# A fourth seven-product pair in the gate and up units of a decoder layer, part of its low halves made by accumulating DMA

## The chip, the cores and the metric

The kernel runs on one core of a Trainium2 chip. The metric is the device time of one execution in microseconds (us); lower is better. A core has a matrix engine (TensorE, in the rows PE; its weight loads are PEld), a vector engine (VectorE, DVE), a scalar engine (ScalarE, ACT), a general engine (GpSimd, POOL) and a queue engine (SyncE, SP). Each takes its own instructions in the order in which the program lists them. They wait for each other by semaphores. Data comes from device memory by DMA, which SP, POOL or ACT start. A kernel keeps its data in an on-chip memory of 128 partitions, and matmuls write into 8 banks of a second memory, each 128 x 512 in fp32.

## What is computed

One decoder layer for 256 rows of width 2048: two token mixers in parallel, an output projection with a residual, and a SwiGLU block (width 5632) with a residual. What the change touches is the SwiGLU block:

```python
h = x + merged_mixers @ w_out
hn = rms_norm(h) * norm_ffn
g, u = hn @ w_ffn_gate, hn @ w_ffn_up          # 2048 x 5632 each
y = h + (silu(g) * u) @ w_ffn_down             # 5632 x 2048
```

All is fp32. Products are made on TensorE in a rounded format, three matmuls for one product: `a_hi*w_hi + a_hi*w_lo + a_lo*w_hi`. A `hi` is a rounded copy, and `lo` is the value minus its `hi`.

## The kernel before

The output projection and the SwiGLU block run as a list (`stream`) of items of class `Pair`, line 1027. A pair is two blocks of 128 rows of two weight columns of 512: four blocks `raw[:, 0..3]`, 1 MB, loaded by two DMAs on SP (`load`, 512 KB each). A **plain** pair (`mm_plain`) multiplies them with the two halves of the rows in 8 products, 24 matmuls. A **seven-product** pair (`mm_seven`) first makes four sums of blocks on VectorE (lines 1052 to 1055) and needs 7 products, 21 matmuls: m1, m2, m3 on the blocks themselves, m4 to m7 on the sums.

`split` makes the operands. A plain pair has one part: `hi` of 2048 columns on ScalarE (line 1060), then `lo` on VectorE (line 1062). A seven-product pair has two parts: three raw blocks (1536 columns), and the four sums (2048). Parts are numbered; a part writes one of four pairs of `hi8`/`lo8` buffers in turn, so it has to wait until TensorE is done with the part four places before it. `run_ffn`, called once ahead of each item, queues loads and parts, so that at most four parts (`PARTS`), those of the running item among them, stand ahead.

A **gate/up unit** (`gate_up(f, hooks)`, f = 0 to 10) is 8 pairs, one pair of rows of the weights after the other, for 512 columns of gate and of up. Pairs 0, 2 and 4 are seven-product ones (`SH`; in f = 0 only 0 and 2). A **down unit** multiplies the product of three or four gate/up units with `w_ffn_down`. The order is f = 0 to 3, two down units of 6 pairs, f = 4 to 7, two down units, f = 8 to 10, two down units.

The banks: m1, m5, m7, m6 take the four `acc` banks; m2, m4, m3 and the bank `c` of the plain pairs take the four others (tag `m`). After the last seven-product pair of a unit `combine` (lines 1118 to 1122) reads the `acc` banks on ScalarE and VectorE; its last instruction is the last to read m5. At the unit's end `last` (line 1131, four instructions) adds the other four banks, and these are free for the next unit only then. In the next unit's first pair m2 is the fifth product, after 12 matmuls. For gate/up, ScalarE applies Silu (1212) and VectorE multiplies (1214).

The product of unit f is transposed for the down unit by `hid_pair` (8 small matmuls, line 1012, into two `acc` banks, then `put_seven` or `put_plain`, which read them and make `hi` and `lo`). Before, this stands in the middle of item 5 of the unit after. With f counted from its group's start, `put_seven` falls to f = 0, 1 of the first group and 0, 1, 2 of the others.

Of the kernel before, what the change touches and what calls it, by code (L numbers as in the profile page):

```python
# [8 lines left out]
F32 = mybir.dt.float32  # L9
# [45 lines left out]
def hybrid_block(ctx: ExitStack, tc: tile.TileContext, x, norm_attn, w_in, fox_f_bias,  # L55
# [893 lines left out]
    hss = keep.tile([P, NT, 4], F32, name="hss")  # L949
    SH = (0, 2, 4)  # L950

# [31 lines left out]
    def put_seven(dst, b, gains):  # L983

        d0, d1 = (dst[:, o].rearrange("p o t -> p (o t)") for o in range(2))
# [12 lines left out]
        nc.vector.tensor_tensor(fo[:, 3], bo[:, 2], fo[:, 2], op=ALU.add)  # L998
        nc.vector.tensor_tensor(d1[:, 0:512], b, d0[:, 0:512].bitcast(F32), op=ALU.subtract)
        if gains is None:  # L1000
            nc.scalar.activation(d0[:, 512:1024], f, AF.Copy)
        else:
            nc.vector.tensor_copy(d0[:, 512:1024], f)
        nc.vector.tensor_tensor(d1[:, 512:1024], f, d0[:, 512:1024].bitcast(F32), op=ALU.subtract)

# [21 lines left out]
    class Pair:  # L1027
        def __init__(self, unit, kp, seven, srcs, mm, pre=None, mid=None, done=None, need=None):
            self.unit, self.kp, self.seven, self.srcs, self.mm = unit, kp, seven, srcs, mm
            self.pre, self.mid, self.done, self.need = pre, mid, done, need  # L1030
            self.parts = 2 if seven else 1
            self.hold = False
            self.raw = None
            self.op = []
# [32 lines left out]

    def unit(order, sevens, srcs, act, done, need, hooks=None, add=None):

# [17 lines left out]
        def mm_seven(ch):  # L1087
            a = act(ch.kp)
            o0 = a.shape[2] - 7

            for key in ("m1 m2 m3 m5 m7 m6 m4" if seen else "m1 m5 m7 m6 m2 m4 m3").split():
                o, part, slot_ = {"m1": (0, 0, 0), "m2": (1, 0, 1), "m3": (6, 0, 2), "m4": (2, 1, 3),
                                  "m5": (3, 1, 0), "m6": (5, 1, 2), "m7": (4, 1, 1)}[key]
                hi, lo = ch.op[part]
# [19 lines left out]
        def combine():  # L1114

            (t1, t3), (u, w) = ([wk([P, 512], "qs", 4) for _ in range(2)], [p3([P, 512], "q2", 5) for _ in range(2)])
# [86 lines left out]
    def hid_pair(f, a, g):  # L1203
# [43 lines left out]
    for g, (f0, f1) in enumerate(GROUPS):  # L1247
# [54 lines left out]

    def run_ffn(i):

# [3 lines left out]
        while True:  # L1308
# [81 lines left out]
```

## Time and profile before

| what | value |
|---|---|
| time, median of 3 runs | 1435.89 us (1435.48 to 1436.24) |
| the profiled execution's own time | 1435.63 us |
| its span, first to last instruction | 1433.9 us |
| TensorE busy in the span | 1424.8 us (99%), 6757 matmuls |
| VectorE busy | 1135.3 us (79%); 88 to 93% in each 100 us from 800 to 1400 us |
| ScalarE busy | 758.7 us (53%) |
| GpSimd busy | 64.9 us (5%) |
| granted TensorE clock | 1.000 over the span |
| DMA | 287.07 MB, mean 200 GB/s |

The profile is of one execution. A busy TensorE there says only that matmuls overlap: a 512-column matmul lasts 0.39 us in the record while the next one starts 0.23 us after it. What it costs is the distance from one start to the next. Idle time of an engine is listed with what ended it.

### The profile page before, as it was taken

What the parts mean: (1) busy time and instruction counts of PE and PEld (TensorE: products, weight loads), DVE (VectorE), ACT (ScalarE), POOL (GpSimd) and SP (SyncE); (2) the same over time, 40 slices, a digit from 0 to 9 for tenths busy, and PEclk for the clock granted to TensorE, in tenths of its full rate; (3) what the DMA queues carried; (4) which work ended last, traced back from release to release, by engine and by line L of the source; (5) the groups of instructions that cost most, each with busy time, mean ns of one, the idle gap of its engine ahead of it and who ended that gap; (6) DMA issues with size and microseconds to landing.
All of it is one profiled execution on the core that took longest, in us unless ns stands there. A gap on an engine that the chain in (4) does not pass through costs nothing.

```text
span 1433.9 us, 18119 instructions
## 1 busy us (share of the span) xinstructions
PE 1424.8 (99%) x6757; PEld 1197.8 (84%) x6757; DVE 1135.3 (79%) x1458; ACT 758.7 (53%) x945; POOL 64.9 (5%) x82
## 2 busy tenths in 40 slices
PE   9999999999999999999999999999999999999998
PEld 7878888899888888888888888888888888888887
DVE  6785866786677545569898999888999988989985
ACT  5466564455566544445565555455555545455542
POOL 0201010000000000000110000010000000000000
PEclk9999999999999999999999999999999999999999
DMA  7567876457544566667775666578555677865594
GB/s 272 185 197 216 268 239 191 145 147 214 152 119 131 178 191 191 190 215 207 249 238 176 206 205 212 199 206 256 190 184 193 204 217 224 240 200 181 180 269 134
DMA packets 156196, 287.07 MB, mean 200 GB/s; under 512 B 9630, under 2 KB 32764, under 8 KB 155980
## 3 DMA queue, kind: packets, MB, share of 16 engines
q1 hardware_dynamic: 150396, 273.77, 60.2%
q0 software_dynamic: 5536, 11.87, 4.3%
q8 instruction: 53, 0.87, 0.2%
q10 hardware_dynamic: 176, 0.27, 0.1%
q14 instruction: 35, 0.29, 0.1%
HBM read 277.48 MB, written 8.40 MB: 199 GB/s over the span
## 4 chain that ended last, share of the span: by engine, by line
PE 93%; DVE 4%; ACT 1%; issue 1%; POOL 0%; ACTq 0%; POOLq 0%; DVEq 0%
PE m L1083 14%; PE m L1085 14%; PE m L1084 14%; PE acc L194 12%; PE acc L196 12%; PE acc L195 12%; PE acc L1084 3%; PE acc L1085 3%; PE acc L1083 3%; PE acc L1012 1%; DVE lo L172 1%; DVE lo L1062 1%; PE m L546 1%; PE m L547 1%; ACT hi L1060 1%
## 5 line engine op out<-in xcount | busy, mean ns | idle before, releaser
L172 DVE TENSOR_TENSOR lo<-raw,hi 128x1024 fp32r<-128x1024 f32 (+5 forms) x229 | 267.5, 1172 | 139.6 <-ACT hi L171 138.8
L1062 DVE TENSOR_TENSOR lo<-raw,hi 128x2048 fp32r<-128x2048 f32 (+1 forms) x148 | 309.7, 2094 | 40.3 <-ACT hi L1060 40.2
L1060 ACT ACTIVATE hi<-raw 128x2048 fp32r<-128x2048 f32 (+1 forms) x148 | 259.6, 1758 | 131.5 <-PE m L1085 67.1
L194 PE MATMUL acc<-hi,u 128*128 128x512 f32 (+4 forms) x832 | 322.3, 387 | 0.7 <-ACT u L271 0.7
L195 PE MATMUL acc<-lo,u 128*128 128x512 f32 (+4 forms) x832 | 317.0, 381 | 1.4 <-DVE lo L172 1.4
L196 PE MATMUL acc<-hi,u 128*128 128x512 f32 (+4 forms) x832 | 316.9, 381 | 0.0
L171 ACT ACTIVATE hi<-raw 128x1024 fp32r<-128x1024 f32 (+5 forms) x229 | 229.0, 1018 | 145.6 <-PE acc L196 135.5
L195 PEld LDWEIGHTS acc<-lo,u 128*128 128x128 f32 x832 | 156.4, 188 | 27.8 <-DVE lo L172 3.1
L196 PEld LDWEIGHTS acc<-hi,u 128*128 128x128 f32 x832 | 156.2, 188 | 27.7 <-DVE u L272 1.1
L194 PEld LDWEIGHTS acc<-hi,u 128*128 128x128 f32 x832 | 156.3, 188 | 26.2 <-ACT u L271 1.2
L1060 ACT ACTIVATE hi<-sums 128x2048 fp32r<-128x2048 f32 x53 | 101.7, 1918 | 140.7 <-DVE sums L1055 126.1
L1083 PE MATMUL m<-hi,hp 128*128 128x512 f32 x440 | 172.1, 391 | 0.0
L1085 PE MATMUL m<-hi,hp 128*128 128x512 f32 x440 | 171.3, 389 | 0.0
L1084 PE MATMUL m<-lo,hp 128*128 128x512 f32 x440 | 171.2, 389 | 0.0
L1062 DVE TENSOR_TENSOR lo<-sums,hi 128x2048 fp32r<-128x2048 f32 x53 | 121.5, 2292 | 27.2 <-ACT hi L1060 27.2
L1085 PEld LDWEIGHTS m<-hi,hp 128*128 128x128 f32 x440 | 82.6, 188 | 17.2
L1084 PEld LDWEIGHTS m<-lo,hp 128*128 128x128 f32 x440 | 82.7, 188 | 16.8
L1083 PEld LDWEIGHTS m<-hi,hp 128*128 128x128 f32 x440 | 82.6, 188 | 16.9
L1083 PE MATMUL m<-hi,u 128*128 128x512 f32 x215 | 84.1, 391 | 0.0
L1085 PE MATMUL m<-hi,u 128*128 128x512 f32 x215 | 83.7, 389 | 0.0
L1084 PE MATMUL m<-lo,u 128*128 128x512 f32 x215 | 83.7, 389 | 0.0
L1052 DVE TENSOR_TENSOR sums<-raw 128x1024 f32<-128x1024 f32 x53 | 64.5, 1217 | 0.2
(307 smaller groups left out, 1963.6 us busy)
## 6 DMA issues: line engine op xcount, KB each, us to landing
raw<-in_w_in_dram SPq DMA_DIRECT2D x127, 512.0 KB
raw<-in_w_ffn_gate_dram SPq DMA_DIRECT2D x88, 512.0 KB
raw<-in_w_ffn_up_dram SPq DMA_DIRECT2D x88, 512.0 KB
raw<-in_w_ffn_down_dram SPq DMA_DIRECT2D x88, 512.0 KB
raw<-in_w_out_dram SPq DMA_DIRECT2D x32, 512.0 KB
raw<-in_w_in_dram SPq DMA_DIRECT2D x24, 384.0 KB
raw<-in_w_up_fox_dram SPq DMA_DIRECT2D x16, 512.0 KB
raw<-in_w_up_nsa_dram SPq DMA_DIRECT2D x16, 512.0 KB
```

The lines of the kernel that those rows point to most:

```text
L171: nc.scalar.activation(hi[:, :m], ch.raw[:, :m], AF.Copy)
L172: nc.vector.tensor_tensor(lo[:, :m], ch.raw[:, :m], hi[:, :m].bitcast(F32), op=ALU.subtract)
L194: nc.tensor.matmul(o, h, ch.hi[:, j], start=first and j == 0, stop=False)
L195: nc.tensor.matmul(o, h, ch.lo[:, j], start=False, stop=False)
L196: nc.tensor.matmul(o, l, ch.hi[:, j], start=False, stop=last and j == w - 1)
L546: nc.tensor.matmul(o, s, ch.hi[:, j], start=j == 0, stop=False)
L1052: nc.vector.tensor_tensor(s[:, 0:2], w[:, 0].unsqueeze(1).to_broadcast([P, 2, 512]), w[:, 1:4:2], op=ALU.add)
L1060: nc.scalar.activation(h, src, AF.Copy)
L1062: return lambda: nc.vector.tensor_tensor(l, src, h.bitcast(F32), op=ALU.subtract)
L1083: nc.tensor.matmul(o, h, hi, start=n == 0, stop=False)
L1084: nc.tensor.matmul(o, h, lo, start=False, stop=False)
L1085: nc.tensor.matmul(o, l, hi, start=False, stop=n + 1 == total[key])
```

## The change

Gate/up units from f = 1 on get a fourth seven-product pair (6), and their items run in the order 0, 1, 2, 3, 4, 6, 5, 7. Of the four plain pairs left, three (1, 3, 7: `thin`) get half of their low part in another way: ScalarE writes the negated rounded copy of the two up blocks into `lo`, and POOL starts a DMA that adds the weights onto it (512 KB, read a second time). VectorE makes only the other half (1024 columns). The second half of such a pair's matmuls needs what the DMA brings.

The `hi` of the sums is made in two instructions of 1024 columns. In a seven-product pair that isn't a unit's first, `run_ffn` is called once more between the first three products and the rest (`between`), and counts the first part as done. The gate product (line 1237 after) is put two items later. The transposes stand ahead of item 7, no longer in the middle of item 5. `put_seven` makes two differences in one instruction and the first `lo` earlier. Buffers are resized.

```diff
-    SH = (0, 2, 4)
+    SH = (0, 2, 4, 6)
...
     def put_seven(dst, b, gains):
-        nc.scalar.activation(d0[:, 0:512], b, AF.Copy)
-        nc.vector.tensor_tensor(fo[:, 1], bo[:, 1], bo[:, 0], op=ALU.subtract)
-        nc.vector.tensor_tensor(fo[:, 0], bo[:, 3], bo[:, 0], op=ALU.subtract)
-        nc.vector.scalar_tensor_tensor(fo[:, 2], fo[:, 0], -1.0, bo[:, 1], op0=ALU.mult, op1=ALU.subtract)
+        nc.scalar.activation(d0[:, 0:n], b[:, 512 - n:], AF.Copy)
+        nc.vector.tensor_tensor(fo[:, 0:2], bo[:, 1:4:2], bo[:, 0].unsqueeze(1).to_broadcast([P, 2, P]),
+                                op=ALU.subtract)
+        nc.vector.scalar_tensor_tensor(fo[:, 2], fo[:, 1], -1.0, bo[:, 1], op0=ALU.mult, op1=ALU.subtract)
+        nc.vector.tensor_tensor(d1[:, 0:n], b[:, 512 - n:], d0[:, 0:n].bitcast(F32), op=ALU.subtract)
         nc.vector.tensor_tensor(fo[:, 3], bo[:, 2], fo[:, 2], op=ALU.add)
-        nc.vector.tensor_tensor(d1[:, 0:512], b, d0[:, 0:512].bitcast(F32), op=ALU.subtract)
...
             h, l = hi[:, :m], lo[:, :m]
-            nc.scalar.activation(h, src, AF.Copy)
+            if src is self.sums:
+                for o in (0, 2):
+                    nc.scalar.activation(hi[:, o:o + 2], src[:, o:o + 2], AF.Copy)
+            elif self.thin:
+                nc.scalar.activation(lo[:, 0:4:3], src[:, 0:4:3], AF.Copy, scale=-1.0)
+                nc.gpsimd.dma_start(lo[:, 0:4:3], self.srcs[1].rearrange("(k p) n -> p k n", p=P), accum_op=ALU.add)
+                src, h, l = src[:, 1:3], hi[:, 1:3], lo[:, 1:3]
+                nc.scalar.activation(hi, self.raw, AF.Copy)
+            else:
+                nc.scalar.activation(h, src, AF.Copy)
...
+                if key == "m5" and later and ch.between:
+                    ch.between()
...
+            stt(u, bk["m5"], -1.0, u, op0=ALU.mult, op1=ALU.subtract)
             stt(w, bk["m5"], -1.0, t3, op0=ALU.mult, op1=ALU.subtract)
-            stt(u, bk["m5"], -1.0, u, op0=ALU.mult, op1=ALU.subtract)
...
     def swiglu(f):
         def done(c):
...
-            for t in range(NT):
-                nc.vector.scalar_tensor_tensor(c[t, 1], c[t, 1], rh[:, t:t + 1], c[t, 0], op0=ALU.mult, op1=ALU.mult)
+            def mult():
+                for t in range(NT):
+                    nc.vector.scalar_tensor_tensor(c[t, 1], c[t, 1], rh[:, t:t + 1], c[t, 0],
+                                                   op0=ALU.mult, op1=ALU.mult)
             hsrc[f] = [c[t, 1] for t in range(NT)]
+            after.append((here[0] + 2, mult))
...
     def gate_up(f, hooks):
-        unit(range(8), SH if f else SH[:2], lambda kp: [w[kp * 2 * P:(kp + 1) * 2 * P, f * 512:(f + 1) * 512]
+        unit((0, 1, 2, 3, 4, 6, 5, 7) if f else range(8), SH if f else SH[:2], lambda kp: [w[kp * 2 * P:(kp + 1) * 2 * P, f * 512:(f + 1) * 512]
                                                         for w in (w_ffn_gate, w_ffn_up)],
-             lambda kp: hT[kp], swiglu(f), None, hooks)
+             lambda kp: hT[kp], swiglu(f), None, hooks, thin=(1, 3, 7) if f else ())
...
-            gate_up(f, transposes(f - 1, 5) if f > f0 + (1 if g else 0) else
+            gate_up(f, transposes(f - 1, (7, 0)) if f > f0 + (1 if g else 0) else
...
-    def run_ffn(i):
+    def run_ffn(i, halfway=False):
...
-                out_parts = sum(1 for (q, _) in parts[:npart] if q >= i)
+                out_parts = sum(1 for (q, o) in parts[:npart] if q > i or (q == i and not (halfway and o == 0)))
...
+        if i >= ffn:
+            ch.between = lambda i=i: run_ffn(i, True)
+        for at_i, fn in [x for x in after if x[0] <= i]:
+            fn()
```

The first place is VectorE at the end of unit f = 5. `acc` and `F` rows up to `u` are the put, `m` rows are `last`, and `lo` rows are parts of the next unit's first pairs. Before:

```order
L1062 TENSOR_TENSOR lo_1712_8989<-raw_1700_8917,hi_1711_8988 128x1536
L995 TENSOR_TENSOR F_9018<-F_9017 128x128
L996 TENSOR_TENSOR F_9018<-F_9017 128x128
L997 SCALAR_TENSOR_TENSOR F_9018<-F_9018,F_9017 128x128
L998 TENSOR_TENSOR F_9018<-F_9017,F_9018 128x128
L999 TENSOR_TENSOR u_1716_9016<-F_9017,u_1716_9016 128x512
L1004 TENSOR_TENSOR u_1716_9016<-F_9018,u_1716_9016 128x512
L974 TENSOR_TENSOR u_1626_8460<-acc_9028,u_1626_8460 128x512
L1062 TENSOR_TENSOR lo_1721_9048<-sums_8990,hi_1720_9047 128x2048
L1062 TENSOR_TENSOR lo_1723_9076<-raw_1703_8948,hi_1722_9075 128x2048
L1131 TENSOR_TENSOR qs_8972<-m_8829,qs_8972 128x512
```

The same place after, from the last instruction of `combine` on:

```order
L1137 SCALAR_TENSOR_TENSOR q_1731_9101<-acc_8887,qs_9099 128x512
L1074 TENSOR_TENSOR lo_1733_9108<-sums_9077,hi_1732_9107 128x2048
L997 TENSOR_TENSOR F_9143<-F_9142 128x256
L999 SCALAR_TENSOR_TENSOR F_9143<-F_9143,F_9142 128x128
L1000 TENSOR_TENSOR u_1735_9141<-F_9142,u_1735_9141 128x512
L1001 TENSOR_TENSOR F_9143<-F_9142,F_9143 128x128
L1006 TENSOR_TENSOR u_1735_9141<-F_9143,u_1735_9141 128x512
L975 TENSOR_TENSOR u_1637_8515<-acc_9152,u_1637_8515 128x512
L1074 TENSOR_TENSOR lo_1740_9160<-raw_1720_9042,hi_1739_9159 128x1024
L1146 TENSOR_TENSOR qs_9098<-m_8899,qs_9098 128x512
```

The put has moved behind the `lo` of the next unit's first sums, and between it and `last` stands one `lo` of 1024 columns where two of 2048 stood.

The second place is ScalarE at the same end of the unit. Before:

```order
L988 ACTIVATE F_9017<-acc_9011 128x512
L994 ACTIVATE u_1716_9016<-F_9017 128x512
L1001 ACTIVATE u_1716_9016<-F_9018 128x512
L973 ACTIVATE u_1626_8460<-acc_9028 128x512
L1060 ACTIVATE hi_1720_9047<-sums_8990 128x2048
L1060 ACTIVATE hi_1722_9075<-raw_1703_8948 128x2048
L1212 ACTIVATE qs_8972<-qs_8972,rh 128x512
```

After, where the rows of line 1067 are the negated copies ahead of the two accumulating DMAs (of pair 7, and of pair 1 of the next unit):

```order
L1067 ACTIVATE lo_1722_9058<-raw_1709_8960 128x2x512
L1070 ACTIVATE hi_1721_9057<-raw_1709_8960 128x2048
L1072 ACTIVATE hi_1724_9075<-raw_1715_8997 128x1536
L1133 ACTIVATE qs_9098<-acc_8883 128x512
L1065 ACTIVATE hi_1732_9107<-sums_9077 128x1024 x2
L990 ACTIVATE F_9142<-acc_9136 128x512
L996 ACTIVATE u_1735_9141<-F_9142 128x512
L1003 ACTIVATE u_1735_9141<-F_9143 128x512
L974 ACTIVATE u_1637_8515<-acc_9152 128x512
L1067 ACTIVATE lo_1740_9160<-raw_1720_9042 128x2x512
L1070 ACTIVATE hi_1739_9159<-raw_1720_9042 128x2048
L1233 ACTIVATE qs_9098<-qs_9098,rh 128x512
```

Ahead of the put stand three more splits, and the negated copy for the next unit's pair 1, with the DMA that it releases, has come to stand behind the put.

## Rows read from the trace of the kernel before

**Rows 1.** TensorE's waits from 800 us on: for what, us, times, longest
```profile
PE acc L1084 <- DVE lo L1062: 0.4, 1, 0.4
```
**Rows 2.** Unit f = 6: us, busy PE, PEld, DVE, ACT, POOL; clock, DMA, GB/s
```profile
1049.80:1092.20 42.40, 42.40 (x193) 35.20 (x192) 39.74 (x38) 23.09 (x18) 0.00 (x0) 1.00 0.60 199
```
**Rows 3.** TensorE's timeline in unit f = 5: start, us, line, tile, count
```profile
1027.91 0.39 PE L1083 MATMUL acc<-hi,h 128*128 128x512 f32 x1
...
1035.39 1.03 PE L1012 MATMUL acc<-ident,q 128*128 128x128 f32 x8
...
1036.50 0.40 PE L1084 MATMUL m<-lo,hp 128*128 128x512 f32 x1
...
1045.57 0.39 PE L1085 MATMUL m<-hi,hp 128*128 128x512 f32 x1
```
**Rows 4.** VectorE's timeline: a combine, a plain part, the sums of a pair
```profile
990.84 0.68 DVE L1119 TENSOR_TENSOR q<-acc,qs 128x512 f32<-128x512 f32 x1
...
993.49 2.28 DVE L1062 TENSOR_TENSOR lo<-raw,hi 128x2048 fp32r<-128x2048 f32 x1
995.68 1.21 DVE L1052 TENSOR_TENSOR sums<-raw 128x1024 f32<-128x1024 f32 x1
...
998.27 1.75 DVE L1062 TENSOR_TENSOR lo<-raw,hi 128x1536 fp32r<-128x1536 f32 x1
```
**Rows 5.** VectorE's timeline at the end of unit f = 5; brackets: idle before
```profile
1039.75 1.75 DVE L1062 TENSOR_TENSOR lo<-raw,hi 128x1536 fp32r<-128x1536 f32 x1
1041.42 0.28 DVE L995 TENSOR_TENSOR F<-F 128x128 f32<-128x128 f32 x1
...
1042.27 0.29 DVE L998 TENSOR_TENSOR F<-F,F 128x128 f32<-128x128 f32 x1
...
1043.26 0.69 DVE L1004 TENSOR_TENSOR u<-F,u 128x512 fp32r<-128x512 f32 x1
1043.87 0.69 DVE L974 TENSOR_TENSOR u<-acc,u 128x512 fp32r<-128x512 f32 x1
1045.55 2.29 DVE L1062 TENSOR_TENSOR lo<-sums,hi 128x2048 fp32r<-128x2048 f32 x1 [1.00 <-ACT hi L1060]
...
1049.96 1.28 DVE L1131 TENSOR_TENSOR qs<-m,qs 128x512 f32<-128x512 f32 x2
```
**Rows 6.** ScalarE's timeline in the same unit
```profile
1028.15 1.92 ACT L1060 ACTIVATE hi<-raw 128x2048 fp32r<-128x2048 f32 x1 [2.31 <-PE m L1085]
...
1042.59 0.63 ACT L1001 ACTIVATE u<-F 128x512 fp32r<-128x512 f32 x1 [5.30 <-DVE F L998]
1043.13 0.58 ACT L973 ACTIVATE u<-acc 128x512 fp32r<-128x512 f32 x1
1043.61 1.91 ACT L1060 ACTIVATE hi<-sums 128x2048 fp32r<-128x2048 f32 x1
...
1050.68 1.34 ACT L1212 ACTIVATE qs<-qs,rh 128x512 f32<-128x512 f32 x2 [3.36 <-DVE qs L1131]
```
**Rows 7.** Groups of 1024 columns, by line and shape: count, busy us, mean ns
```profile
L171 ACT ACTIVATE hi<-raw 128x1024 fp32r<-128x1024 f32 x179 | 187.1, 1057 | 129.8 <-PE acc L196 125.1 <-issue 1.5 <-ACT hi L171 1.4
...
L172 DVE TENSOR_TENSOR lo<-raw,hi 128x1024 fp32r<-128x1024 f32 x179 | 218.4, 1223 | 124.9 <-ACT hi L171 124.2 <-issue 0.2
```
**Rows 8.** GpSimd's timeline: accumulating DMAs of 256 KB into on-chip memory, issue times
```profile
1367.88 0.88 POOL L1154 DMA_DIRECT2D qs<-hacc  x1 [144.85 <-DVE q L1119]
1369.56 0.87 POOL L1154 DMA_DIRECT2D qs<-hacc  x1 [0.80 <-PE acc L1012]
...
1413.72 0.86 POOL L1154 DMA_DIRECT2D qs<-hacc  x1 [41.51 <-DVE q L1119]
1415.17 0.86 POOL L1154 DMA_DIRECT2D qs<-hacc  x1 [0.58 <-DVE q L1121]
```
**Rows 9.** Line 1154 around 1369.56 us: from issue to landing
```profile
DMA to landing us min/median/max: 8.5/8.5/8.5
```
**Rows 10.** Line 1154 around 1415.17 us: from issue to landing
```profile
DMA to landing us min/median/max: 5.8/5.8/5.8
```

More of the change, by code (lines that the diff above doesn't have):

```diff
@@ L983, in put_seven @@
     def put_seven(dst, b, gains):
+        n = (dst.shape[2] - 4) * P
         d0, d1 = (dst[:, o].rearrange("p o t -> p (o t)") for o in range(2))
@@ L993, in put_seven @@
         fo, bo = (v.rearrange("p (o t) -> p o t", o=4) for v in (f, b))
-        nc.scalar.activation(d0[:, 0:512], b, AF.Copy)
-        nc.vector.tensor_tensor(fo[:, 1], bo[:, 1], bo[:, 0], op=ALU.subtract)
-        nc.vector.tensor_tensor(fo[:, 0], bo[:, 3], bo[:, 0], op=ALU.subtract)
-        nc.vector.scalar_tensor_tensor(fo[:, 2], fo[:, 0], -1.0, bo[:, 1], op0=ALU.mult, op1=ALU.subtract)
+        nc.scalar.activation(d0[:, 0:n], b[:, 512 - n:], AF.Copy)
[3 more added lines that the diff above has]
+        nc.vector.tensor_tensor(d1[:, 0:n], b[:, 512 - n:], d0[:, 0:n].bitcast(F32), op=ALU.subtract)
         nc.vector.tensor_tensor(fo[:, 3], bo[:, 2], fo[:, 2], op=ALU.add)
-        nc.vector.tensor_tensor(d1[:, 0:512], b, d0[:, 0:512].bitcast(F32), op=ALU.subtract)
         if gains is None:
-            nc.scalar.activation(d0[:, 512:1024], f, AF.Copy)
+            nc.scalar.activation(d0[:, n:n + 512], f, AF.Copy)
         else:
-            nc.vector.tensor_copy(d0[:, 512:1024], f)
-        nc.vector.tensor_tensor(d1[:, 512:1024], f, d0[:, 512:1024].bitcast(F32), op=ALU.subtract)
+            nc.vector.tensor_copy(d0[:, n:n + 512], f)
+        nc.vector.tensor_tensor(d1[:, n:n + 512], f, d0[:, n:n + 512].bitcast(F32), op=ALU.subtract)
     def transpose_pair(make, srcs, c, kp, sevens, gains=None, where="tp"):
@@ L1031, in __init__ @@
             self.parts = 2 if seven else 1
-            self.hold = False
-            self.raw = None
+            self.hold = self.thin = False
+            self.raw = self.sums = None
+            self.between = None
             self.op = []
@@ L1066, in free, with unit @@
             self.op = []
-    def unit(order, sevens, srcs, act, done, need, hooks=None, add=None):
+    def unit(order, sevens, srcs, act, done, need, hooks=None, add=None, thin=()):
         hooks = hooks or {}
@@ L1089, in mm_seven @@
             o0 = a.shape[2] - 7
-            for key in ("m1 m2 m3 m5 m7 m6 m4" if seen else "m1 m5 m7 m6 m2 m4 m3").split():
+            later = bool(seen)
+            for key in ("m1 m2 m3 m5 m7 m6 m4" if later else "m1 m5 m7 m6 m2 m4 m3").split():
+                if key == "m5" and later and ch.between:
+                    ch.between()
                 o, part, slot_ = {"m1": (0, 0, 0), "m2": (1, 0, 1), "m3": (6, 0, 2), "m4": (2, 1, 3),
-                                  "m5": (3, 1, 0), "m6": (5, 1, 2), "m7": (4, 1, 1)}[key]
+                                  "m5": (4, 1, 0), "m6": (5, 1, 2), "m7": (3, 1, 1)}[key]
                 hi, lo = ch.op[part]
@@ L1114, in combine @@
         def combine():
-            (t1, t3), (u, w) = ([wk([P, 512], "qs", 4) for _ in range(2)], [p3([P, 512], "q2", 5) for _ in range(2)])
+            (t1, t3), (u, w) = ([wk([P, 512], "qs", 4) for _ in range(2)], [p3([P, 512], "q2", 4) for _ in range(2)])
             tt, stt = nc.vector.tensor_tensor, nc.vector.scalar_tensor_tensor
@@ L1145, in unit @@
                                (lambda kp=kp: need(kp)) if need else None))
+            stream[-1].thin = kp in thin
     def two(w, r0, c0):
@@ L1168, in put_h @@
         k = kp // 2 % 2
-        make = lambda kp: p3([P, 2, 8, P], "h7", len(SH), F32R) if kp in SH else p3([P, 2, 2, T], "hp", 8 - len(SH), F32R)
+        make = lambda kp: (p3([P, 2, 2, T], "hp", 4, F32R) if kp % 2 else p3([P, 2, 7, P], "h7", 2, F32R) if kp < 4
+                           else p3([P, 2, 8, P], "h8", 2, F32R))
         gains = [vecT[:, VF + 2 * kp + o:VF + 2 * kp + o + 1] for o in range(2)]
@@ L1207, in hid_pair @@
                                    where="acc")
+    here = [0]
+    after = []
     def swiglu(f):
         def done(c):
+            c = dict(c)
             for t in range(NT):
                 nc.scalar.activation(c[t, 0], c[t, 0], AF.Silu, scale=rh[:, t:t + 1])
-            for t in range(NT):
-                nc.vector.scalar_tensor_tensor(c[t, 1], c[t, 1], rh[:, t:t + 1], c[t, 0], op0=ALU.mult, op1=ALU.mult)
+            def mult():
+                for t in range(NT):
+                    nc.vector.scalar_tensor_tensor(c[t, 1], c[t, 1], rh[:, t:t + 1], c[t, 0],
+                                                   op0=ALU.mult, op1=ALU.mult)
             hsrc[f] = [c[t, 1] for t in range(NT)]
+            after.append((here[0] + 2, mult))
         return done
@@ L1230, in transposes @@
     def transposes(f, j):
-        return {(j, 1): lambda: [hid_pair(f, o, g_of[f]) for o in range(2)]}
+        return {j if isinstance(j, tuple) else (j, 1): lambda: [hid_pair(f, o, g_of[f]) for o in range(2)]}
     def gate_up(f, hooks):
-        unit(range(8), SH if f else SH[:2], lambda kp: [w[kp * 2 * P:(kp + 1) * 2 * P, f * 512:(f + 1) * 512]
+        unit((0, 1, 2, 3, 4, 6, 5, 7) if f else range(8), SH if f else SH[:2], lambda kp: [w[kp * 2 * P:(kp + 1) * 2 * P, f * 512:(f + 1) * 512]
                                                         for w in (w_ffn_gate, w_ffn_up)],
-             lambda kp: hT[kp], swiglu(f), None, hooks)
+             lambda kp: hT[kp], swiglu(f), None, hooks, thin=(1, 3, 7) if f else ())
     def down_unit(g, i, order, hooks):
@@ L1330, in hybrid_block @@
     for i, ch in enumerate(stream):
+        here[0] = i
         if i < ffn:
@@ L1336, in hybrid_block @@
             run_ffn(i)
+        if i >= ffn:
+            ch.between = lambda i=i: run_ffn(i, True)
+        for at_i, fn in [x for x in after if x[0] <= i]:
+            fn()
+        after[:] = [x for x in after if x[0] > i]
         if ch.need:
```

## The prediction

> **What bounds the kernel now.** I began with TensorE's waits, because only time in which TensorE stands still, or matmuls that go away, can change the end. From 800 us on it waited once, for 0.4 us [rows 1]. So the SwiGLU block lasts as long as its matmuls take to start one after the other: from 1036.50 to 1045.57 us there are 40 distances, 0.2267 us each [rows 3]. Eight transposes take 1036.50 - 1035.39 less one distance, 0.88 us. Next I read the stretch of one whole gate/up unit: 42.40 us, of which VectorE works 39.74 and ScalarE 23.09 [rows 2]. So VectorE has 2.7 us of slack in a unit, and it can't use all of it: 1.00 us of idle time stands in one place ahead of the `lo` of the sums, which waits for ScalarE's `hi` [rows 5]. The reader is to see that TensorE is the bound and VectorE is close behind it. What matters is whether VectorE still delivers on time at each place, not how busy it is on average.
>
> **What the change removes.** Ten units (f = 1 to 10) have one pair more at 21 instead of 24 matmuls: 30 x 0.2267 = 6.80 us. This lies wholly on the path. Against the profiled execution's own time of 1435.63 us it gives 1428.8 if nothing waits.
>
> **VectorE's load.** A seven-product pair costs it 2.59 us of sums [rows 4], 1.67 for the `lo` of 1536 columns (1039.75 to 1041.42) [rows 5] and 2.2 for the `lo` of the sums, 6.46 together; a plain part costs 2.19 (993.49 to 995.68) [rows 4]. A thin part has 1024 columns, mean 1.22 us [rows 7]; starts stand some 0.09 closer than durations, so 1.13. Per unit: one plain part becomes a seven-product pair (+4.27), three become thin (-3.18), net +1.1. The two later changes to the put nearly cancel. So VectorE works some 40.8 us in a unit that now has 180 matmuls and 8 transposes, 41.7 us. On average it fits, if idle time stays under 0.9 us a unit. ScalarE gets three copies of 1024 columns (1.06 each [rows 7]) and one more `hi` pair, about 5 us in all, and has 18 us of slack [rows 2]. Splitting the `hi` of the sums lets its second half end under the `lo` of 1536 columns, so idle time ahead of the `lo` of the sums (1.00 us in [rows 5]) goes; that helps VectorE and costs nothing. The later gate product is 1.3 us of VectorE's work moved to where VectorE is ahead; nobody waits for it until the transposes, six items on.
>
> **The unit's end.** This is the place where I expect the new wait. Part numbers give a closed chain there. Pair 7's part takes the buffer of pair 4's sums, which TensorE leaves when item 5 begins. From that moment, in us:
>
> - 0.24 until ScalarE starts (1027.91 to 1028.15) [rows 3, 6]; 0.95 for the negated copy (1.06 less the overlap); 1.94 from the start of `hi` to VectorE's `lo` (1043.61 to 1045.55) [rows 5, 6]; 1.13 for that `lo`. Sum 4.26.
> - Next unit's pair 0, first part: 2.59 + 1.67. Sum 8.52.
> - `combine` 2.65 (990.84 to 993.49) [rows 4]. Sum 11.17. `lo` of the sums 2.20. Sum 13.37.
> - The put up to its last `F`: 1.14 before (1041.42 to 1042.56) [rows 5], plus 0.61 for the `lo` that now stands inside, less 0.20 for the merged instruction, 1.55. Sum 14.92.
> - ScalarE: 0.03, then 0.54 and 0.48 for the two copies of the put [rows 6]. Sum 15.97. The negated copy of the next unit's pair 1, 0.95, its `hi` 1.94, and VectorE's `lo` 1.13, which stands ahead of `last`. Sum 19.99.
> - The first instruction of `last`, until another engine may go on: 0.72 (1049.96 to 1050.68) [rows 5, 6]. Sum 20.71.
>
> TensorE needs for the same way, from item 5 to the fifth product of the next unit, which wants the bank that `last` frees: 21 + 24 + 24 + 12 matmuls, 18.36 us, and 0.88 for the transposes, 19.24. So it comes 1.47 us early and waits. Before, the put stood 8 us further ahead, `last` began at 1049.96, 0.16 us after the unit's end, and the bank was free some 2 us before it was wanted [rows 2, 5].
>
> Behind the waiting matmul all of TensorE is queued; no other engine profits. The chain holds in the six units whose end has a `put_seven`: f = 1, 2, 5, 6, 9, 10. 6 x 1.47 = 8.8 us. In f = 3 and 7 the put is plain and the next unit has no thin pair, so `last` is on time; but there too the second transposes want the bank of m5, which the end of `combine` frees at 11.17 + 0.1, and TensorE is there after 21 + 24 matmuls and half the transposes, 10.6. 2 x 0.67 = 1.3 us. In f = 4 and 8 there is no put, the `lo` of pair 1 is ready early, and nothing waits. The errors of the terms (the strided copy, the reordered put, `combine` with its last two exchanged) may add up to 0.8 us either way in a chain, so I bound this part by 4 and 15 us and take 10.1.
>
> **The accumulating DMA.** No row shows one of 512 KB. The nearest rows are two of 256 KB, one after the other: at 1367.88 and 1369.56, while loads run, the second lands 8.5 later, 10.2 after the first was issued; at 1413.72 and 1415.17, near the end, 5.8 later, 7.3 after the first [rows 8 to 10]. I take the middle, 8.7, since loads run beside it but the DMA share is 0.60 [rows 2]. The time at hand, from the negated copy to the lo matmul of the pair's second half: pair 7 12.8 us; pair 3 10.0 (8.9 where the unit began late); pair 1 behind a put, 17.0 to 25.7 on the scale above, 8.7. So pair 7 is safe, pair 3 mostly, pair 1 of f = 2, 3, 6, 7 and 10 sits on the edge. I take 0.2 us for these five, 1.0 us, with bounds 0 (7.3) and 13 (10.2: 5 x 1.5 and 5 x 1.2). GpSimd's issue costs 0.9 us here [rows 8] and hides, as its queue is empty but for the writes after down units; there pair 3 of f = 4 and 8 queues behind four of them, still inside its 10 us.
>
> The Trainium skill, "DMA: Bandwidth & Descriptors", section "Anatomy of one DMA — SWDGE (gpsimd) path", gives 2.0 us plus the bytes over 436 GB/s for a DMA from this queue, an estimate of 3.2 us for 512 KB. The rows above have 5.8 us and more for half as much, so the trace does not bear it out beside the loads. By the page the term for the DMA would be 0 and the sum 1438.9.
>
> **Sum.** 1435.63 - 6.80 + 8.8 + 1.3 + 1.0 = 1439.9. The median of the runs stands 0.26 above the profiled execution, so 1440.
>
> **Rivals.**
> *All waits hidden.* If the chain is shorter by some 1.5 us (the copies overlap more, VectorE comes to `combine` earlier), TensorE never waits and the time is 1428.8 to 1433. For it: the average fits, 40.8 of 41.7, and the two units without a put have slack. Against it: each link is a measured row and is anchored at TensorE's own release, so a faster start elsewhere doesn't shorten it.
> *The DMA is late.* If 512 KB beside loads take 10.2 us or more, pairs 1 and 3 wait in most units: 8 to 13 us on top, 1447 to 1455. It decides from 8.7 us on for pair 1 and from 10 for pair 3. For it: the load of another 1 MB falls into the same stretch. Against it: the share of 0.60 leaves room, and a late pair 1 gives pair 3 time.
> *The chain is real but half as long*, 0.7 us a unit: 1434 to 1436, no difference. This is the lower part of my own case.
>
> **How the numbers follow.** The forecast's case (1434 to 1446) gets 0.43, of which 0.18 lies within 0.2% of 1435.89 (1433.0 to 1438.8, about what a measurement of this kernel can tell from no change) and 0.25 above. All hidden: 0.32, faster. DMA late: 0.25, slower. So faster 0.32, same 0.18, slower 0.50. Faster and slower both hold much, so the likeliest case's own range is 1434 to 1446; the range for 8 in 10 goes from the floor, 1428, to 1452, which leaves out the worse half of the late DMA.
>
> **What would show it.** The matmul count falls by 30, and VectorE's busy time rises by about 11 us. Right: TensorE waits of 0.5 to 2 us for line 1146, six times, and for line 1137 eight times at most; `lo` of 1024 columns starting after the unit's last matmul. DMA: landings of 512 KB at 7 to 10 us, and TensorE waits for `lo` by DMA. Wrong: no waits at the unit's end and a span of about 1427; or VectorE idle under 0.5 us a unit with TensorE waiting for its `lo` everywhere, which would mean that the load, not the place, decides.

## The result, and the profile after

| | time, us | span of the profiled execution |
|---|---|---|
| before | 1435.86 median of 5 (1435.36 to 1436.24) | 1433.9 |
| after | 1446.80 median of 5 (1445.88 to 1448.47) | 1445.1 |

The ratio is 1.008, interval 1.0065 to 1.0094: the changed kernel is 11 us slower. The time lies in the range of 8 in 10 (1428 to 1452), 6.8 us above the predicted one and 0.8 above the range that the likeliest case gave itself (1434 to 1446). The page of after, span and engines (busy us, share, instructions):

```profile
span 1445.1 us, 18346 instructions
...
PE 1422.4 (98%) x6727; PEld 1192.6 (83%) x6727; DVE 1143.9 (79%) x1488; ACT 813.8 (56%) x1049; POOL 100.8 (7%) x112
```

The 30 matmuls are gone (6757 to 6727), VectorE works 8.6 us more and ScalarE 55. What came instead stands in TensorE's waits from 700 us on (for what: us, times, longest), the view of [rows 1]:

```profile
PE m L1095 <- DVE qs L1146: 9.5, 7, 1.8
PE m L1096 <- DMA lo<-in_w_ffn_up_dram: 2.0, 2, 1.6
PE acc L1014 <- DVE q L1134: 1.2, 1, 1.2
PE acc L1014 <- ACT qs L1133: 0.9, 1, 0.9
```

Before had one wait of 0.4 there. The first row is the forecast one: TensorE wants the bank that `last` (line 1146) frees. VectorE's timeline in after at the end of unit f = 5, the place of [rows 5]:

```profile
1041.07 1.22 DVE L1074 TENSOR_TENSOR lo<-raw,hi 128x1024 fp32r<-128x1024 f32 x1 [0.44 <-ACT hi L1070]
1042.21 1.22 DVE L1055 TENSOR_TENSOR sums<-raw 128x1024 f32<-128x1024 f32 x1
...
1046.47 0.68 DVE L1134 TENSOR_TENSOR q<-acc,qs 128x512 f32<-128x512 f32 x1
...
1049.12 2.28 DVE L1074 TENSOR_TENSOR lo<-sums,hi 128x2048 fp32r<-128x2048 f32 x1
1051.31 0.42 DVE L997 TENSOR_TENSOR F<-F 128x256 f32<-128x256 f32 x1
...
1052.58 0.28 DVE L1001 TENSOR_TENSOR F<-F,F 128x128 f32<-128x128 f32 x1
1053.56 0.69 DVE L1006 TENSOR_TENSOR u<-F,u 128x512 fp32r<-128x512 f32 x1 [0.70 <-ACT u L1003]
...
1056.80 1.23 DVE L1074 TENSOR_TENSOR lo<-raw,hi 128x1024 fp32r<-128x1024 f32 x1 [1.94 <-ACT hi L1070]
1057.94 1.28 DVE L1146 TENSOR_TENSOR qs<-m,qs 128x512 f32<-128x512 f32 x2
```

The last two rows are the loss. VectorE stands idle for 1.94 us, ahead of a `lo` that it can't make yet, while `last`, which needs nothing from ScalarE, stands behind it. Before, `last` stood at 1049.96, 0.16 us after the unit's end [rows 2, 5], and nobody waited for it. ScalarE in after over the same stretch shows what the `lo` waits for: the put's copy, then the negated copy, then the `hi`:

```profile
1052.90 0.63 ACT L1003 ACTIVATE u<-F 128x512 fp32r<-128x512 f32 x1 [2.59 <-DVE F L1001]
...
1053.91 1.05 ACT L1067 ACTIVATE lo<-raw 128x1024 fp32r<-128x1024 f32 x1
1054.86 1.90 ACT L1070 ACTIVATE hi<-raw 128x2048 fp32r<-128x2048 f32 x1
```

And TensorE in after, which should have gone on at 1057.45 and does so 1.23 us later:

```profile
1057.22 0.39 PE L1097 MATMUL acc<-hi,h 128*128 128x512 f32 x1
1058.68 0.50 PE L1095 MATMUL m<-hi,h 128*128 128x512 f32 x1 [1.06 <-DVE qs L1146]
1059.01 0.40 PE L1096 MATMUL m<-lo,h 128*128 128x512 f32 x1
```

Where the profiled execution's 11.2 us more of span went, each wait as the distance between two matmul starts less the normal one:

| place | us |
|---|---|
| 30 matmuls fewer | -6.80 |
| ends of f = 1, 2, 5, 6, 9, 10: 1.24, 1.66, 1.23, 1.70, 1.23, 1.97 | 9.03 |
| end of the second down unit, ahead of f = 4 | 1.59 |
| accumulating DMA of pair 3 in f = 4 and f = 8: 1.80, 0.55 | 2.35 |
| transposes in f = 0, and in the first of the last two down units | 1.04 + 1.39 |
| matmuls at the lower clock behind the wait of 1.97 | 1.5 |
| sum | 10.1 |

Some 1.1 us is left (1.5, if the 0.4 of [rows 1], gone in after, is counted as a gain). About 1.0 of it stands right behind the waits: the 512-column matmul that ends a wait is followed by the next one after 0.33 to 0.34 us instead of 0.2267 (1058.68 and 1059.01 above), at each of the nine places where one waited (the seven ends and the two DMAs). The rest is not placed.

### The profile page after: what moved, and what is told of

It is laid out like the page before. It is cut to its first block, busy times and chain, and to the rows that moved or that the text cites. A ratio compares the mean times of both kernels' runs of the same rounds, so it can differ in the third digit from the quotient of the medians.

```text
span 1445.1 us, 18346 instructions
## 1 busy us (share of the span) xinstructions
PE 1422.4 (98%) x6727; PEld 1192.6 (83%) x6727; DVE 1143.9 (79%) x1488; ACT 813.8 (56%) x1049; POOL 100.8 (7%) x112
## 4 chain that ended last, share of the span: by engine, by line
PE 73%; DVE 15%; issue 4%; ACT 3%; DMA 3%; SPq 0%; POOL 0%; ACTq 0%; DVEq 0%; POOLq 0%
PE acc L194 12%; PE acc L196 12%; PE acc L195 12%; PE m L1096 9%; PE m L1095 9%; PE m L1097 8%; DVE lo L1074 6%; PE acc L1096 2%; PE acc L1097 2%; PE acc L1095 2%; DVE sums L1055 2%; DMA lo<-in_w_ffn_up_dram 1%; ACT hi L1070 1%; DVE sums L1057 1%; DMA raw<-in_w_ffn_up_dram 1%
## 5 line engine op out<-in xcount | busy, mean ns | idle before, releaser
L1074 DVE TENSOR_TENSOR lo<-raw,hi 128x1536 fp32r<-128x1536 f32 (+2 forms) x148 | 271.7, 1844 | 48.6 <-ACT hi L1072 26.4
L1072 ACT ACTIVATE hi<-raw 128x1536 fp32r<-128x1536 f32 (+1 forms) x118 | 198.5, 1684 | 101.6 <-PE m L1097 48.5
L1065 ACT ACTIVATE hi<-sums 128x1024 fp32r<-128x1024 f32 x126 | 130.7, 1058 | 116.8 <-DVE sums L1055 60.2
L1074 DVE TENSOR_TENSOR lo<-sums,hi 128x2048 fp32r<-128x2048 f32 x63 | 144.0, 2285 | 11.9 <-ACT hi L1065 11.8
L1096 PE MATMUL m<-lo,hp 128*128 128x512 f32 x352 | 137.2, 390 | 2.0 <-DMA lo<-in_w_ffn_up_dram 2.0
L1095 PE MATMUL m<-hi,hp 128*128 128x512 f32 x352 | 137.9, 392 | 0.0
L1097 PE MATMUL m<-hi,hp 128*128 128x512 f32 x352 | 137.1, 389 | 0.0
L1055 DVE TENSOR_TENSOR sums<-raw 128x1024 f32<-128x1024 f32 x63 | 76.7, 1218 | 3.8 <-DMA raw<-in_w_ffn_up_dram 2.8
L1096 PEld LDWEIGHTS m<-lo,hp 128*128 128x128 f32 x352 | 66.1, 188 | 16.3 <-DMA lo<-in_w_ffn_up_dram 2.9
L1097 PEld LDWEIGHTS m<-hi,hp 128*128 128x128 f32 x352 | 66.1, 188 | 13.7
L1095 PEld LDWEIGHTS m<-hi,hp 128*128 128x128 f32 x352 | 66.1, 188 | 13.5
```

Of the source, the lines that this page charges most:

```text
L1065: nc.scalar.activation(hi[:, o:o + 2], src[:, o:o + 2], AF.Copy)
L1095: nc.tensor.matmul(o, h, hi, start=n == 0, stop=False)
L1096: nc.tensor.matmul(o, h, lo, start=False, stop=False)
L1097: nc.tensor.matmul(o, l, hi, start=False, stop=n + 1 == total[key])
```

## Experiments

Two theories stood against each other. **Place**: the order on VectorE and ScalarE at a unit's end makes `last` late, and that is the loss. **Load**: VectorE simply has too much to do. A third, the **DMA**, was to be priced beside them. Each ratio is against the kernel before, on the same chip in the same job (medians 1435.93, 1435.78 and 1435.9).

### Put the next unit's low part behind `last`

An item with `hold` keeps a low part that fills the fourth place back until its own work is issued (the list `late`); before, one item of the kernel used it. Here the last item of each gate/up and down unit does.

```diff
     def gate_up(f, hooks):
...
+        stream[-1].hold = True
...
     def down_unit(g, i, order, hooks):
...
+        stream[-1].hold = True
```

> The low part of the next unit's first thin (or plain) pair is put behind the four instructions of `last` on VectorE, in every gate/up and down unit; nothing else moves. Theory (place): `last` no longer waits for the scalar engine's copies of that part, its first instruction comes some 16.7 + 0.7 = 17.4 us after the buffer is freed, ahead of the 19.2 us at which TensorE wants the bank. The six waits of 1.2 to 2.0 us at the ends of f = 1, 2, 5, 6, 9, 10 and the one of 1.6 us ahead of f = 4 go (10.6 us), and with them the stretch at a lower clock behind the longest one (1.5 us): about 1434.5 us, 1432 to 1437. Rival (load): VectorE has too much work in a unit, moving one instruction only moves the wait; TensorE then waits for `lo` in pairs 1 and 2 instead, and the time stays at 1443 to 1447.

Measured: 1434.59 us (1433.45 to 1436.22), ratio 0.9991 [0.9981, 1.0000]. That is 12.2 us less than after; the seven waits at a unit's end (10.6) and the stretch at the lower clock (1.5) make 12.1. That the two agree to 0.1 is partly chance, since the other waits moved as well and nearly cancel: 1.5 us less for the DMA, 1.9 more for a `lo` in the first of the last two down units, 0.5 more for the copy of m1. VectorE of this kernel at the end of f = 5:

```profile
1048.86 0.68 DVE L975 TENSOR_TENSOR u<-acc,u 128x512 fp32r<-128x512 f32 x1
1049.46 1.28 DVE L1146 TENSOR_TENSOR qs<-m,qs 128x512 f32<-128x512 f32 x2
1050.65 1.28 DVE L1146 TENSOR_TENSOR q<-m,q 128x512 f32<-128x512 f32 x2
1051.85 1.21 DVE L1074 TENSOR_TENSOR lo<-raw,hi 128x1024 fp32r<-128x1024 f32 x1
```

`last` now runs where VectorE was idle, and the `lo` behind it finds its `hi` done. No instruction was taken from VectorE, so this is place and not load. TensorE's waits of this kernel from 700 us on:

```profile
PE acc L1096 <- DVE lo L1074: 1.5, 2, 1.2
PE acc L1014 <- ACT qs L1133: 1.4, 1, 1.4
PE acc L1014 <- DVE q L1134: 1.2, 1, 1.2
PE m L1096 <- DMA lo<-in_w_ffn_up_dram: 0.7, 1, 0.7
```

### Make all low halves on VectorE

The changed kernel, with this edit alone:

```diff
-             lambda kp: hT[kp], swiglu(f), None, hooks, thin=(1, 3, 7) if f else ())
+             lambda kp: hT[kp], swiglu(f), None, hooks)
```

> The changed kernel without thin pairs: all low halves on VectorE, no accumulating DMA, no negated copies. VectorE gets 3 x 1.06 = 3.2 us more per unit, some 44 us of work for 41.7 us of matmuls. Place: the chain at the unit's end stays about as long (two low parts longer by 1.06 each, two negated copies of 0.95 shorter), but over three or four units in a row VectorE falls behind by up to 2.3 us each: 1450 to 1465 us, with TensorE waits for `lo`. Rival (the DMA and the copies that feed it cost more than they save): faster than 1446.8, down to 1440, since the two late DMAs (2.4 us) and the copies ahead of `last` are gone.

Measured: 1457.84 us (1456.94 to 1458.0), ratio 1.0150 [1.0133, 1.0167]. It lies where place and load both put it; the rival, that the accumulating DMA is the loss, falls: without it the kernel is 11 us slower again. Place and load are not told apart by this run alone. It showed the clock, though. TensorE of this kernel at the end of f = 5:

```profile
1061.28 0.39 PE L1097 MATMUL acc<-hi,h 128*128 128x512 f32 x1
1064.38 0.50 PE L1095 MATMUL m<-hi,h 128*128 128x512 f32 x1 [2.71 <-DVE qs L1146]
...
1065.86 0.63 PE L1097 MATMUL m<-hi,h 128*128 128x512 f32 x1
```

Behind the wait of 2.71 us matmuls last 0.63 instead of 0.39 us, some eight of them; the same stands behind the waits at 825.52 and 1321.62.

### The order inside the put

The changed kernel, with this edit alone:

```diff
-        nc.vector.tensor_tensor(d1[:, 0:n], b[:, 512 - n:], d0[:, 0:n].bitcast(F32), op=ALU.subtract)
         nc.vector.tensor_tensor(fo[:, 3], bo[:, 2], fo[:, 2], op=ALU.add)
+        nc.vector.tensor_tensor(d1[:, 0:n], b[:, 512 - n:], d0[:, 0:n].bitcast(F32), op=ALU.subtract)
```

> Only the order inside `put_seven` is that of before: the second F difference ahead of the first low part, so that the scalar engine's copy of F starts 0.6 us earlier and runs beside that low part. Theory (place): the chain is 0.6 us shorter in each of seven ends of units, 4 us in all: 1442 to 1443.5 us, each wait for line 1146 shorter by 0.6 us. Rival (load): VectorE's own work is the same and the waits elsewhere stay: 1445.5 to 1447.

Measured: 1442.92 us (1442.42 to 1445.66), ratio 1.0052 [1.0037, 1.0067]. TensorE's wait for `last` in this kernel:

```profile
PE m L1095 <- DVE qs L1146: 5.9, 7, 1.5
```

In after it is 9.5: 3.6 us over seven places, 0.51 each (1.24 became 0.75, 1.70 became 1.16). So the put's last `F` does lie on the chain, and the `lo` that the change moved ahead of it costs nearly its 0.61 us each time. The matmuls at the lower clock are gone too, where the wait is now 1.62. These two make 5.1 us, and the time fell by 3.9, about the 4 that were expected: a new wait of 1.34 for a `lo`, at 1368.21, took most of the rest back. So the theory's chain is borne out, and the agreement of the total is partly chance.

### One accumulating DMA fewer in f = 4 and 8

On top of the kernel with the late low part, pair 3 is not thin in the two units where its DMA came late:

```diff
-             lambda kp: hT[kp], swiglu(f), None, hooks, thin=(1, 3, 7) if f else ())
+             lambda kp: hT[kp], swiglu(f), None, hooks, thin=(1, 7) if f in (4, 8) else (1, 3, 7) if f else ())
```

> As the run with the late low part, and pair 3 of f = 4 and of f = 8 isn't thin (its low part all on VectorE), because there the accumulating DMA queues behind the four writes of a down unit. Theory: the two waits for that DMA (1.8 and 0.55 us) go as well: 2 us less than the run with the late low part alone, about 1432.5 us. Rival: VectorE, with 1.06 us more in these two units, makes TensorE wait for it instead: the same as the run with the late low part alone.

Measured: 1434.5 us (1432.83 to 1435.59), ratio 0.9986 [0.9977, 0.9995], a miss: 1432.5 was expected. The wait for the DMA is gone and one for VectorE, 0.91 us at 992.10, has taken its place. TensorE's waits in this kernel for a `lo`:

```profile
PE acc L1096 <- DVE lo L1074: 2.2, 3, 1.2
```

The `lo` that VectorE gets back is 1.07 us longer and there is no room for it there.

### Where else the split by parts puts work

In f = 0 and the down units no pair is thin; this run leaves `between` to units that have thin pairs (with the late low part):

```diff
-                if key == "m5" and later and ch.between:
+                if key == "m5" and later and thin and ch.between:
```

> As the run with the late low part, but parts are queued in the middle of a pair in gate/up units f = 1 to 10 only, no longer in the output projection, in f = 0 and in the down units. Theory: there the extra call puts scalar-engine copies ahead of the copy of m1 and vector-engine low parts ahead of `combine`, and so the transposes of that unit wait for their bank: the waits of 1.5 us at 748, 1.4 us at 1360 and 1.4 us at 1367 us go, the one of 0.8 us for the DMA stays: some 4 us less than 1434.6, 1430 to 1431.5. Rival (these waits come from the later place of the put of pairs 4 to 6 and from the work of a seven-product pair 6): no change, 1434 to 1435.

Measured: 1432.0 us (1431.04 to 1433.42), ratio 0.9973 [0.9961, 0.9985], 2.6 us below the kernel with the late low part, where some 4 were expected, and 0.5 above the expected range. The waits of transposes for lines 1133 and 1134 are gone. The third wait that was to go, at 1360, was one for a `lo` and stayed (1.35 at 1357.99); the one for the DMA, which was to stay, went. In after the first of them reads, on ScalarE and then on TensorE:

```profile
745.17 1.92 ACT L1072 ACTIVATE hi<-raw 128x2048 fp32r<-128x2048 f32 x1 [1.23 <-DMA raw<-in_w_ffn_up_dram]
746.99 0.57 ACT L1133 ACTIVATE qs<-acc 128x512 f32<-128x512 f32 x1
...
747.62 0.66 PE L1014 MATMUL acc<-ident,qs 128*128 128x128 f32 x4 [0.88 <-ACT qs L1133]
```

The copy of m1, which frees a bank, stands behind a `hi` that `between` had queued ahead of it and that itself had waited 1.23 us for its load. It is the same pattern as at the unit's end, on another engine.

### All three together

The three edits above in one kernel: the late low part, `between` for units with thin pairs alone, and the put's old order.

```diff
+        stream[-1].hold = True
...
-                if key == "m5" and later and ch.between:
+                if key == "m5" and later and thin and ch.between:
...
-        nc.vector.tensor_tensor(d1[:, 0:n], b[:, 512 - n:], d0[:, 0:n].bitcast(F32), op=ALU.subtract)
         nc.vector.tensor_tensor(fo[:, 3], bo[:, 2], fo[:, 2], op=ALU.add)
+        nc.vector.tensor_tensor(d1[:, 0:n], b[:, 512 - n:], d0[:, 0:n].bitcast(F32), op=ALU.subtract)
```

> As the run before it, with the order inside `put_seven` of the kernel before. Theory: with the low part late the chain at the unit's end has 1.8 us to spare, so 0.6 us less there is worth nothing: the same within 0.7 us. Rival (VectorE's idle time of 0.7 us per put still counts, since units follow each other): 3 to 4 us faster.

Measured: 1429.76 us (1429.62 to 1432.78), ratio 0.9963 [0.9949, 0.9977]: the fastest kernel of the study, 6.1 us below before and 17.0 below after. It came out 2.2 us below the run ahead of it, where at most 0.7 was expected and 3 to 4 by the rival; so it lies between the two theories, and as the intervals of the two ratios overlap, the size of the difference is not sure. The two profiled executions differ by 1.3; of this the waits make 0.5 (1.35 and 0.49 there, 1.36 here), and gaps of at most 0.11 us each make some 0.6. TensorE's waits of this kernel from 700 to 1430 us, all of them:

```profile
PE acc L1096 <- DVE lo L1074: 1.2, 1, 1.2
```

Taking the span of before, less 6.80, less the 0.4 of [rows 1], plus 1.36 (the one wait, as a distance), gives 1428.1; its span is 1428.0. So the change's whole gain is there once nothing waits, and no time is left over. VectorE's load is that of after. Unit f = 6, from its fifth product to that of the next unit, in after and then in this kernel (us; busy PE, PEld, DVE, ACT, POOL; clock, DMA share, GB/s):

```profile
1058.70:1102.20 43.50, 41.96 (x189) 34.52 (x189) 40.43 (x41) 28.22 (x27) 3.58 (x3) 1.00 0.78 229
```
```profile
1049.35:1091.05 41.70, 41.70 (x190) 34.63 (x189) 40.55 (x41) 28.38 (x28) 3.58 (x3) 1.00 0.80 239
```

The same 41 instructions of VectorE, 40.4 and 40.6 us of work; in the one TensorE stands still for 1.5 us, in the other never.

### No split by parts at all

With the late low part:

```diff
-                if key == "m5" and later and ch.between:
+                if False:
```

> As the run with the late low part, without any queueing in the middle of a pair. Theory: in gate/up units `combine` then stands ahead of the next pair's sums on VectorE and waits for the last matmul of pair 6, 1.2 us of idle time, still inside what the end of the unit has to spare; the waits in f = 0 and the last down units go as in the run with queueing in thin units alone: 1430 to 1433. If queueing by parts of a pair is what keeps VectorE on time in gate/up units, it is slower than 1434.6.

Measured: 1431.99 us (1430.77 to 1434.12), ratio 0.9975 [0.9964, 0.9985], the same as with `between` in the gate/up units (1432.0). So with the late low part in place, queueing by parts gives nothing in the gate/up units, and it costs where no pair is thin.

### The gate product at once

The run with `between` for thin units, and line 1237 issued at the unit's end again:

```diff
-            after.append((here[0] + 2, mult))
+            mult()
```

> As the run with queueing in thin units alone, with the gate product put at once again, right behind `last` and ahead of the late low part. Theory: the late low part comes 1.3 us later, some 0.3 us after TensorE wants it, and VectorE waits up to 0.7 us for Silu: 1 to 3 us slower than that run. Rival (the later place of the product is worth nothing): the same within 0.7 us.

Measured: 1435.86 us (1434.29 to 1438.11), ratio 1.0001 [0.9991, 1.0010]: 3.9 us slower, where 1 to 3 were expected. TensorE waits 0.27 to 0.30 us for a `lo` at the end of five units with a put and 1.10 us at the sixth (f = 10), and three times for an accumulating DMA:

```profile
PE m L1096 <- DMA lo<-in_w_ffn_up_dram: 2.3, 3, 1.4
```

So putting the product later is a part of the change that pays, by giving VectorE 1.3 us at the unit's end and letting the part behind it start sooner.

### Pair 6 plain again

The fastest kernel, with three seven-product pairs per unit as before:

```diff
-        unit((0, 1, 2, 3, 4, 6, 5, 7) if f else range(8), SH if f else SH[:2], lambda kp: ...
+        unit((0, 1, 2, 3, 4, 6, 5, 7) if f else range(8), SH[:3] if f else SH[:2], lambda kp: ...
```

> As the best run so far (late low part, queueing by parts in thin units, old order inside the put), but pair 6 of the gate/up units is multiplied as a plain pair again: 30 matmuls more at 0.2267 us. If TensorE's matmuls are the bound of the best run, it is 6.8 us slower, 1436 to 1437, with VectorE idle 4.3 us more per unit and no new waits. If something else (VectorE, DMA) sets the pace of the best run, the difference is smaller, under 4 us.

Measured: 1435.53 us (1435.27 to 1436.15), ratio 0.9998 [0.9988, 1.0008]. TensorE waits nowhere from 700 us on, and the kernel is 5.8 us slower than with the fourth pair: 6.80 for the matmuls, less the 1.36 that the other still waits, makes 5.4. The gain is in the matmuls alone; the rest of the change only makes room for it.

### The fastest kernel without the accumulating DMA

No pair has the number 99, so none is thin, while `between` stays where it is in the fastest kernel:

```diff
-             lambda kp: hT[kp], swiglu(f), None, hooks, thin=(1, 3, 7) if f else ())
+             lambda kp: hT[kp], swiglu(f), None, hooks, thin=(99,) if f else ())
```

> As the best run so far, with all low halves made on VectorE and no accumulating DMA: 3.2 us more of VectorE's work per unit, some 44 us for 41.7 us of matmuls, in runs of three, four and three units. If the average load counts once the place is mended, TensorE waits up to 2.3 us per unit less what the parts ahead cover: 8 to 20 us slower, 1438 to 1450. If only the place counted, within 1.5 us of 1429.8.

Measured: 1443.25 us (1443.03 to 1444.41), ratio 1.0054 [1.0039, 1.0069], 13.5 us slower than with thin pairs. The same 41.70 us in this kernel, columns as above:

```profile
1049.35:1091.05 41.70, 40.30 (x179) 32.42 (x178) 41.16 (x39) 25.52 (x23) 0.00 (x0) 1.00 0.56 181
```

VectorE is all but full (41.16 of 41.70) and TensorE does not get through a whole unit in that time: 179 matmuls where the fastest kernel has 190. TensorE waits in many places for a `lo` and for what the transposes need. So the load theory is right of this kernel, and wrong of after.

## Why the prediction came out as it did

**The bound and the removed matmuls: right.** The fastest kernel and the one with pair 6 plain again show 6.8 us of matmuls on the path, and TensorE as the bound in both.

**VectorE's load: right.** 40.8 us a unit were forecast, with room in 41.7 us; f = 6 of the fastest kernel has 40.55 of 41.70 and keeps TensorE running. The total rose by 8.6 in after and 9.9 in the fastest, for 11.

**The unit's end: right in place, mechanism and size.** Six ends cost 9.03 us, 8.8 were forecast. In the rows of f = 5 above the links lie, from the `hi` at 1039.14 on, at the forecast distances: VectorE's `lo` 1.93 later (1.94), `combine` 7.33 (7.33), the put's `F` 12.17 (12.18), ScalarE's copy 13.76 (13.76), `last` 18.80 (18.80). What was off is the first link: the negated copy starts before item 5 does, not 0.24 behind it, since it overwrites a `lo` alone, and the last matmul to read that is the one before the last. Item 5 starts at 1038.20, and ScalarE at 1038.17:

```profile
1038.17 1.07 ACT L1067 ACTIVATE lo<-raw 128x1024 fp32r<-128x1024 f32 x1 [0.52 <-PE m L1096]
```

The wait there was 1.23, not 1.47. In f = 2 and 6, which follow a unit that began late, ScalarE and VectorE run from one part into the next in pair 7's part, where in f = 5 they idle for 0.52 and 0.44 us, and the waits are 1.66 and 1.70; in f = 10 the `lo` ahead of `last` is that of a plain pair, 2048 columns (2.29 us), and the wait is 1.97. The mean of the six, 1.51, hides this spread: a first link that was too long and three longer ends offset each other, so that the sum came within 0.2 us is partly luck.

**A place left out.** The list of units with a put at their end had only gate/up units. The second down unit ahead of f = 4 has a put in its item 4, the thin `lo` of f = 4's pair 1 stands ahead of its `last`, and it cost 1.59. The step that failed is "The chain holds in the six units"; there are seven.

**The second transposes (1.3 us): wrong.** They never waited for m5's bank. Where transposes wait at a put, it is for line 1134, the first instruction of `combine`, which frees m6's bank; that one comes 2 us earlier. In f = 10 the eight transposes ran from 1345.11, before the last instruction of `combine` began at 1345.85.

**The DMA (1.0 us): the size of one DMA was too long, the place was wrong.** All 30 in after, from issue to landing:

```profile
DMA to landing us min/median/max: 5.7/6.3/10.4
```

The forecast took 8.7 from two DMAs of 256 KB in a row [rows 9, 10]; one of 512 KB is not as slow as two. Those two rows also hid a spread: the eight DMAs of line 1154 in before took from 4.2 to 11.5 us. Pair 1, which I had put on the edge, never waited. The waits came where I had written "still inside its 10 us": pair 3 of f = 4 and 8, behind four writes after a down unit. GpSimd in after there, for f = 4:

```profile
973.13 1.76 POOL L1252 DMA_DIRECT2D hacc<-qs  x2 [2.47 <-DVE qs L1146]
974.32 2.32 POOL L1252 DMA_DIRECT2D hacc<-q  x2
...
979.55 1.20 POOL L1068 DMA_DIRECT2D lo<-in_w_ffn_up_dram  x1 [2.90 <-ACT lo L1067]
```

Issued at 979.55, it is the one that took 10.4, and TensorE went on at 990.01:

```profile
990.01 0.50 PE L1096 MATMUL m<-lo,hp 128*128 128x512 f32 x1 [1.64 <-DMA lo<-in_w_ffn_up_dram]
```

The one of f = 8, issued at 1233.40 behind four such writes, took 10.2; the other 28 took 5.7 to 9.8. No row of the prediction showed a landing behind such writes. That the writes are what makes these two the slowest was not tried apart. The Trainium skill, "DMA: Bandwidth & Descriptors", section "Anatomy of one DMA — SWDGE (gpsimd) path", led to an estimate of 3.2 us for this DMA; the trace does not agree, its shortest being 5.7.

**Not in the sum at all.** The waits of transposes for the copy of m1 and for `combine` (1.04 and 1.39 us): I costed the split by parts at nothing outside the gate/up units. There `between` queues a `hi` early, and what stands behind it on ScalarE is the copy that frees a bank. And the matmuls at the lower clock, below, and the 1.0 us right behind the waits.

Together: +0.2 at the six ends, +1.6 for the seventh, -1.3, +1.35 for the DMA, +2.4 for the transposes, +1.5 for the clock and +1.0 behind the waits make 6.8 of the 6.9 us between the sum and the profiled execution. Of the rivals, "all waits hidden" is what the change does once the order is put right at three places (1429.76, inside its 1428.8 to 1433); "the DMA is late" has nearly the measured time (1447 to 1455) and the wrong reason.

## What to carry to other kernels

When an early operand for the next stage is queued ahead of the instruction that frees a result bank, it can hold the bank back even on an engine with idle time: ask of each moved instruction what it waits for, and who waits behind it on that engine. Here the order of one instruction per unit was worth 12 us, nearly twice the change's gain, while the load was the same. A chain of measured rows anchored at the bound engine's own release gave each wait to within 0.5 us; what such a chain misses is a place not listed, so list every unit's end, of whatever kind, before multiplying.

## What the runs showed of the hardware

The longest wait of after, 1.97 us (1.81 as listed), is followed by slow matmuls. TensorE in after:

```profile
1356.13 0.50 PE L1095 MATMUL m<-hi,u 128*128 128x512 f32 x1 [1.81 <-DVE qs L1146]
...
1356.99 0.63 PE L1095 MATMUL m<-hi,u 128*128 128x512 f32 x1
1357.42 0.63 PE L1096 MATMUL m<-lo,u 128*128 128x512 f32 x1
...
1360.34 0.39 PE L1097 MATMUL m<-hi,u 128*128 128x512 f32 x1
```

The granted clock there, by stretches of after, columns as above:

```profile
1356.10:1358.00 1.90, 1.87 (x6) 1.51 (x7) 1.90 (x4) 1.89 (x3) 0.00 (x0) 0.69 0.66 180
1358.00:1360.40 2.40, 2.40 (x8) 1.87 (x7) 2.33 (x4) 1.43 (x2) 0.00 (x0) 0.53 0.84 294
```

Starts lie 0.43 us apart instead of 0.2267: the level of 1.2 GHz, for some eight matmuls, 1.5 us lost on top of the wait. The same stands behind the waits of 2.4 to 2.9 in the kernel with all low halves on VectorE. Behind the other waits of after, the longest 1.80 (for the DMA, at 990.01), and behind the 1.62 at the same place with the put's old order, the clock stayed. I had counted a wait at its own length; the longest one of after cost 3.5 us, nearly twice that. That the wait brought the lower clock is read from these places alone, and was not tried apart.

A `lo` buffer comes free one matmul before its `hi` (0.23 us, lines 1096 and 1097), and an instruction that writes it alone can start that much sooner (ScalarE at 1038.17, released by line 1096). An accumulating DMA of 512 KB took 6.3 us in the middle beside loads, less than two of 256 KB in a row had let me expect [rows 9, 10].
